# Seven-product v projection: first product in accumulator banks, phased sums of x, weight loads three tiles ahead, another store queue

## The chip, the cores and the metric

The kernel runs on one core of a Trainium2 chip. A core has a matrix engine (PE, with its weight loads PEld), three engines for element-wise work (DVE, ACT, POOL), and SP, which here only issues transfers. Each engine works through its own list of instructions in order and waits on semaphores for the others. The matrix engine writes to eight banks of PSUM of 128 x 512 float32, called bank 0 to 7 below. Transfers between the core's SBUF and DRAM are issued by SP or by ACT. The metric is device time in microseconds (us) of one execution.

## The reference

Two layers of a hybrid backbone run on 256 prompt tokens and 1024 sample tokens, 1280 rows of 1024 columns together, that is ten row tiles of 128. Layer 0 is a state-space mixer beside a convolution module; layer 1 is a chunked gating unit. The change lies at the start of layer 1:

```
u, v, gate = split(h @ w_in, 3)        # h: 1280 x 1024, w_in: 1024 x 6144
v = layer_norm(v)                      # over 2048 columns
s = per chunk and group: c_ws @ v + c_bs
y = (u * s * silu(gate)) @ w_out
x = layer_norm(ALPHA * x + gate_ada * y)
```

Everything is float32. h is x times (1 + scale) plus shift, with x the normalised output of layer 0. The part at hand is `v = h @ w_in[:, 2048:4096]`, 1280 x 1024 times 1024 x 2048, and the per-row statistics of v.

## The kernel before

**Float32 from two halves.** Each operand is split in two fp32r parts: a high part by a copy on ACT, a low part by a subtraction on DVE. A product is three matmuls: high x high, high x low, low x high.

**Seven products for eight.** The v projection uses a Strassen-like scheme (Winograd's form). The rows are halved (row tiles 0 to 4 and 5 to 9), the 1024 columns of x are halved (A11, A12, A22 and so on are such quarters of x), and the weights are taken in two passes p of two column blocks of 512, halved by rows. Each pass has seven products of a quarter, or a sum of quarters, with a weight block, or a difference of blocks, instead of eight. They run in the order `VORD = (1, 2, 5, 6, 7, 4, 3)`. A product is five steps, one for each row tile of the half; a step is 12 matmuls of 128x512 (4 pieces of the inner dimension, three matmuls each). Two passes of seven products of five steps make the loop `for step in range(70)` (line 1599), with m = step // 5 the number of the product and i = step % 5 the row tile. Products 6, 7 and 3 use sums of quarters of x: S2 = A21 + A22 - A11, S3 = A11 - A21 and S4 = A12 - S2, kept as split pairs.

**What a step does besides.** `v_post` (line 1571) takes the step's bank: ACT copies it, DVE adds it to an accumulator. `acc1` is five whole PSUM banks (3 to 7), `acc2` five buffers in SBUF. `mm_bank` hands out banks 0, 1, 2 in turn. Product 1 goes to a bank of `mm_bank`, and ACT copies it into `acc1[i]` (line 1573). Finished pieces of v get their statistics (`v_out`, line 1563, BN_STATS at 1564) and go to DRAM (vD) through ACT's queue (line 1565).

**Weights.** The first two products' weights come through an older stream (`W`, `wV`). For m from 2 to 13 each product has four `Item`s, k = 0 to 3, a 128x512 tile each: `load` (line 1462, SP, one or two sources of 256 KB), `comb` (line 1466, POOL takes the difference of two sources; for products 5 and 6 the difference is also stored to tD by SP, line 1468, since a later product needs it), and `split` (line 1473 ACT, 1474 DVE). A table `sched` puts the split of tile k of product m at step e = 5 (m - 1) + k, its comb at e - 1 and its load at e - 2. The raw tiles use a ring of five buffers, `hraw`.

**Sums of x.** The transposed rows of x were stored to xkD (line 1317) when they were made. `sum_load` and `sum_load2` read the quarters back (1408, 1409, 1412); `sums` (1422) forms S3 and S2 in part on POOL (1426, 1427) and DVE (1428, 1429), stores the fourth sum to sD (1430, SP) and splits S3 (1416, 1417); a second table at line 1627 splits S2. `S4Item` loads sD again and splits S4.

**The order of the work.** All of it is written out by hand: the program order of each engine is the order of the calls in the loop. After a step's matmuls come, in this order, the remaining transposes of row tiles 8 and 9 from layer 0 (`l8` and `l9`: PE line 324 into a bank, ACT line 1305, then POOL 1312 and 1316 and ACT 1315, and the xkD store), `v_post`, the splits, combs and loads of `sched`, and the sums. Waits follow from the buffers that instructions share. Ahead of the loop `fin0` finishes row tile 9 of layer 0: DVE reads its banks at line 1290, after splitting the first v weights at line 261.

## Time and profile before

| | |
|---|---|
| median of three runs | 2160.49 us (2158.58 to 2163.11) |
| profiled execution, its own time | 2159.95 us |
| its span, first to last instruction | 2158.2 us |
| mean granted PE clock | 0.965 |
| PE busy | 2014.7 us, 93% |
| DVE, ACT, POOL busy | 66%, 44%, 49% |
| the stage of the change | 1207.5 to 1481.8 us |

How to read it: the profile records each instruction's start and duration on its engine. Times are us from the span's start. "Idle before, releaser" says how long an engine stood still ahead of an instruction and whose completion ended that. `L209` is the helper that issues every matmul, so matmuls are told apart by the tiles they read. A granted clock of 0.50 means that matmuls ran at half speed. `SPq` and `ACTq` are the queues in which SP and ACT issue transfers; "to landing" is the time from issue to arrival. Names such as Flo, Fhi, Wr, Xa and Xb are buffers in SBUF, S4s is the area in which sums are formed, and ps is PSUM. The row tiles of x are in Rh (high) and Rl (low).

### The profile page before, as it was taken

What the parts mean: (1) busy time and instruction counts of PE and PEld (TensorE: products, weight loads), DVE (VectorE), ACT (ScalarE), POOL (GpSimd) and SP (SyncE); (2) the same over time, 40 slices, a digit from 0 to 9 for tenths busy, and PEclk for the clock granted to TensorE, in tenths of its full rate; (3) what the DMA queues carried; (4) which work ended last, traced back from release to release, by engine and by line L of the source; (5) the groups of instructions that cost most, each with busy time, mean ns of one, the idle gap of its engine ahead of it and who ended that gap; (6) DMA issues with size and microseconds to landing.
All of it is one profiled execution on the core that took longest, in us unless ns stands there. A gap on an engine that the chain in (4) does not pass through costs nothing.

```text
span 2158.2 us, 32301 instructions
## 1 busy us (share of the span) xinstructions
PE 2014.7 (93%) x12032; PEld 1781.0 (83%) x12032; DVE 1430.9 (66%) x2018; ACT 960.1 (44%) x1804; POOL 1050.2 (49%) x982
## 2 busy tenths in 40 slices
PE   7999999998989899899999767989999999989998
PEld 5788888878879788689988545768999999988987
DVE  5777888876795986966656436556555555555566
ACT  3555555567554554655544423333433333331221
POOL 3487788934654646526614433023444444445312
PEclk8999999999989999999999888999999999999999
DMA  8343421366423323244486356554323222265632
GB/s 333 106 137 113 150 77 57 96 191 189 120 73 101 108 78 113 94 152 153 156 274 211 132 194 198 179 183 149 94 93 94 93 94 93 69 226 179 205 129 86
DMA packets 183718, 300.62 MB, mean 139 GB/s; under 512 B 15536, under 2 KB 111992, under 8 KB 183560
## 3 DMA queue, kind: packets, MB, share of 16 engines
q1 hardware_dynamic: 139824, 256.69, 36.8%
q10 hardware_dynamic: 43736, 41.86, 5.7%
q8 instruction: 95, 1.56, 0.3%
q14 instruction: 63, 0.52, 0.1%
HBM read 218.35 MB, written 80.13 MB: 138 GB/s over the span
## 4 chain that ended last, share of the span: by engine, by line
PE 40%; DVE 9%; DMA 4%; POOL 3%; issue 3%; ACT 1%; SPq 1%; ACTq 0%; DVEq 0%; POOLq 0%
PE ps L209 40%; DVE X L914 1%; DVE Fhi L1148 1%; DMA Flo<-tD 1%; DMA Flo<-in_wv 1%; DVE Fhi L1291 1%; DVE Rl L320 1%; POOL Flo L1466 1%; DVE Fhi L901 1%; DVE Fhi L1292 1%; ACT Rh L319 0%; DVE Flo L685 0%; POOL X L865 0%; DVE Fhi L1290 0%; DVE Wr L261 0%
## 5 line engine op out<-in xcount | busy, mean ns | idle before, releaser
L209 PE MATMUL ps<-Rh,Wr 128*128 128x512 f32 (+2 forms) x2688 | 716.0, 352 | 3.9 <-ACT Rh L415 1.4
L209 PEld LDWEIGHTS ps<-Rh,Wr 128*128 128x128 f32 x2688 | 478.8, 193 | 69.2 <-issue 7.5
L209 PE MATMUL ps<-Rl,Wr 128*128 128x512 f32 (+2 forms) x1344 | 462.8, 349 | 1.8 <-DVE Rl L417 1.6
L209 PE MATMUL ps<-Wr,Rh 128*128 128x256 f32 (+2 forms) x1670 | 376.1, 316 | 34.8 <-DVE Fhi L1290 13.8
L596 POOL TENSOR_TENSOR X<-X 128x1295 f32<-128x1295 f32 x96 | 297.5, 3099 | 77.6 <-ACT X L594 72.1
L209 PEld LDWEIGHTS ps<-Wr,Rh 128*128 128x128 f32 x1670 | 276.1, 192 | 56.2 <-ACT Wr L1473 14.3
L209 PEld LDWEIGHTS ps<-Rl,Wr 128*128 128x128 f32 x1344 | 257.3, 192 | 29.9 <-DVE Rl L417 2.7
L209 PE MATMUL ps<-Wr,Rl 128*128 128x256 f32 (+2 forms) x854 | 267.0, 313 | 0.9 <-DVE Rl L320 0.8
L209 PEld LDWEIGHTS ps<-Wr,Rl 128*128 128x128 f32 x854 | 163.3, 191 | 10.6 <-DVE Rl L320 1.3
L590 DVE SCALAR_TENSOR_TENSOR ps<-Fhi,Flo,ps 128x1295 f32<-128x1295 f32 x102 | 160.0, 1569 | 2.9
L209 PE MATMUL ps<-Xa,Rh 128*128 128x512 f32 (+1 forms) x432 | 122.7, 359 | 3.9 <-DVE Xb L1733 2.5
L261 DVE TENSOR_TENSOR Wr<-Flo,Wr 128x1024 fp32r<-128x1024 f32 (+1 forms) x60 | 98.0, 1641 | 42.6 <-ACT Wr L259 42.6
L209 PE MATMUL ps<-Xb,Rh 128*128 128x512 f32 (+1 forms) x456 | 118.9, 350 | 1.3 <-ACT Xb L1473 1.1
L1466 POOL TENSOR_TENSOR Flo<-Flo 128x512 f32<-128x512 f32 x32 | 41.5, 1297 | 149.3 <-DMA Flo<-in_wv 72.4
L1148 DVE SCALAR_TENSOR_TENSOR Fhi<-Fhi,Flo 128x256 f32<-128x256 f32 (+2 forms) x144 | 109.2, 759 | 5.2 <-ACT Fhi L1144 0.8
L594 ACT ACTIVATE X<-Fhi,Flo 128x1295 f32<-128x1295 f32 x78 | 103.5, 1374 | 13.4 <-ACT Fhi L643 7.5
L220 POOL TENSOR_SCALAR Flo<-Flo 128x1 f32<-128x1 f32 (+1 forms) x31 | 11.9, 385 | 192.6 <-DVE Flo L686 186.6
L914 DVE SCALAR_TENSOR_TENSOR X<-X,Flo 128x128 f32<-128x128 f32 x160 | 92.5, 636 | 5.3 <-ACT X L911 3.6
L1528 ACT ACTIVATE Wr<-Flo 128x512 fp32r<-128x512 f32 x72 | 44.9, 624 | 114.8 <-PE ps L209 101.5
L209 PE MATMUL ps<-Xa,Rl 128*128 128x512 f32 (+1 forms) x252 | 91.5, 363 | 4.3 <-DVE Rl L320 4.3
L1529 DVE TENSOR_TENSOR Wr<-Flo,Wr 128x512 fp32r<-128x512 f32 x72 | 73.3, 1018 | 27.3 <-ACT Wr L1528 27.3
L209 PEld LDWEIGHTS ps<-Xa,Rh 128*128 128x128 f32 x432 | 77.4, 193 | 16.4 <-issue 2.8
(350 smaller groups left out, 4137.2 us busy)
## 6 DMA issues: line engine op xcount, KB each, us to landing
Fhi<-abD SPq DMA_DIRECT2D x80, 256.0 KB, 3.4
Fhi<-in_ada SPq DMA_DIRECT2D x34, 512.0 KB, 8.0
Flo<-in_wv SPq DMA_DIRECT2D x64, 256.0 KB, 3.7
Flo<-in_wug SPq DMA_DIRECT2D x32, 512.0 KB, 3.3
Flo<-in_wB SPq DMA_DIRECT2D x24, 512.0 KB, 3.3
Xb<-vD SPq DMA_DIRECT2D x15, 640.0 KB, 4.3
pD<-Xb SPq DMA_DIRECT2D x26, 320.0 KB, 2.5
Flo<-in_wA SPq DMA_DIRECT2D x16, 512.0 KB, 3.4
```

The lines of the kernel that those rows point to most:

```text
L209: PE.matmul(out=out, lhsT=a, rhs=b, start=st, stop=sp)
L261: e.tensor_tensor(out=l_, in0=r, in1=h_.bitcast(F32), op=SUB)
L320: eng.tensor_tensor(out=rl, in0=src, in1=rh.bitcast(F32), op=SUB)
L590: V.scalar_tensor_tensor(out=aD[:, 0:n], in0=u[:, k:k + n], scalar=wc(k), in1=aD[:, 0:n], op0=MULT, op1=ADD)
L594: S.activation(out=o[:, 0:n], in_=u[:, k:k + n], func=AF.Copy, scale=wc(k))
L596: G.tensor_tensor(out=aP[:, 0:n], in0=aP[:, 0:n], in1=o[:, 0:n], op=ADD)
L901: V.scalar_tensor_tensor(out=a[:, q], in0=a[:, q2], scalar=nA[:, sl(1, c)][:, h:h + 1], in1=a[:, q], op0=ADD, op1=MIN)
L914: V.scalar_tensor_tensor(out=cbd[:, q], in0=cbfb[:, 128:256], scalar=dt[:, sl(1, c)][:, h:h + 1], in1=cbd[:, q], op0=MULT, op1=ADD)
L1148: V.scalar_tensor_tensor(out=ob[:, a:e], in0=ib[:, a + k:e + k], scalar=w4(k), in1=ob[:, a:e], op0=MULT, op1=ADD)
L1466: G.tensor_tensor(out=self.r[0], in0=self.r[0], in1=self.r[1], op=SUB)
L1528: S.activation(out=w[:, 0:512], in_=src, func=AF.Copy)
L1529: V.tensor_tensor(out=w[:, 512:1024], in0=src, in1=w[:, 0:512].bitcast(F32), op=SUB)
```

## The change

Four things are changed, all in the loop of 70 steps.

- Product 1 is written straight into `acc1[i]`; its copy on ACT is gone, and `mm_bank` is not asked in those steps. The transposes of row tile 8 move from steps 1 and 2 to steps 2 and 3, those of row tile 9 from steps 3 and 4 to 6 and 7. The area for the sums is set up after step 7 instead of 4, and three statistics that were taken before it exists are copied over.
- The sums run in phases with tables of their own: `sum_load`, `sum_load2`, `sums` (POOL), `sums2` (DVE, and the split of S3), `sums3` (the sD store, and the split of S2). The fourth quarter of a round gets one of four places instead of a single one.
- The raw weight tiles are a first-in, first-out list: `load` takes buffers from its head, `split` gives them back. Two more buffers join at step 10. From m = 4 on a load is issued three steps ahead of its split, and its comb two steps.
- The store of a difference to tD is issued by ACT, after the split's copy, instead of SP.

```diff
+            def quarter(i):
+                m_ = 2560 + i % 2 * 1024
+                l_ = (4608, 2048, 4608, 0, 512)[i]
+                return (st[:, m_:m_ + 512], st[:, m_ + 512:m_ + 1024], st[:, i * 512:(i + 1) * 512], st[:, l_:l_ + 512])
+
             def sum_load(i):
...
             def sum_load2(i):
-                SP.dma_start(out=st[:, 4608:5120], in_=xkD[i, :, 512:1024])
+                a12 = quarter(i)[3]
+                SP.dma_start(out=a12, in_=xkD[i, :, 512:1024])
...
             def sums(i):
...
+                m0, m1, a11, _ = quarter(i)
                 G.tensor_tensor(out=m1, in0=m0, in1=m1, op=ADD)
                 G.tensor_tensor(out=m0, in0=a11, in1=m0, op=SUB)
+
+            def sums2(i):
+                m0, m1, a11, a12 = quarter(i)
                 V.tensor_tensor(out=a11, in0=m1, in1=a11, op=SUB)
                 V.tensor_tensor(out=a12, in0=a12, in1=a11, op=SUB)
+                to_sum(S3, i, m0)
+
+            def sums3(i):
+                _, _, a11, a12 = quarter(i)
                 SP.dma_start(out=sD[i], in_=a12)
-                to_sum(S3, i, m0)
+                to_sum(S2, i, a11)
...
                 def load(self):
-                    self.r = [next_raw() for _ in self.src]
+                    self.r = [hraw.pop(0) for _ in self.src]
...
                 def comb(self):
                     if len(self.r) == 2:
                         G.tensor_tensor(out=self.r[0], in0=self.r[0], in1=self.r[1], op=SUB)
-                        if self.keep is not None:
-                            SP.dma_start(out=self.keep, in_=self.r[0])
 
                 def split(self):
...
                     S.activation(out=h[:, c], in_=self.r[0], func=AF.Copy)
+                    if self.keep is not None:
+                        S.dma_start(out=self.keep, in_=self.r[0])
                     V.tensor_tensor(out=l[:, c], in0=self.r[0], in1=h[:, c].bitcast(F32), op=SUB)
+                    hraw.extend(self.r)
...
-                    self.r = next_raw()
+                    self.r = vtmp[self.i % 2]
                     SP.dma_start(out=self.r, in_=sD[self.i])
...
-                    at(e - 1, it.comb)
-                    at(e - 2, it.load)
-            for i, e in enumerate((19, 24, 26, 28, 29)):
+                    at(e - (1 if m < 4 else 2), it.comb)
+                    at(e - (2 if m < 4 else 3), it.load)
+            for i, e in enumerate((27, 28, 29, 30, 31)):
...
-                if j == 1:
-                    S.activation(out=acc1[i], in_=b, func=AF.Copy)
-                elif j == 2:
+                if j == 2:
...
+            vsv = F[:, FB - 70:FB - 52].rearrange("p (t n s) -> p t n s", n=1, s=6)
             for step in range(70):
...
+                    Wr.put(5 * WS, 6 * WS, (5 * WS, WS, sb.tile([128, WS], F32, name="Wr5f", tag="Wr5")))
+                    hraw += [Wr[:, 5 * WS + q * 512:5 * WS + 512 + q * 512] for q in range(2)]
...
-                b = mm_bank()
+                b = acc1[i] if j == 1 else mm_bank()
...
-                if step in (1, 2):
-                    l8(mm_bank, (step - 1,))
-                if step in (3, 4):
-                    l9(mm_bank, (step - 3,))
+                if step in (2, 3):
+                    l8(mm_bank, (step - 2,))
+                if step in (6, 7):
+                    l9(mm_bank, (step - 6,))
                 v_post(p, j, i, b[:, :])
-                if step == 4:
+                if step == 7:
                     st = sums_area()
...
-                for q in {11: (0, 1), 13: (2,), 15: (3,), 17: (4,)}.get(step, ()):
-                    to_sum(S2, q, st[:, q * 512:(q + 1) * 512])
-                if step in (7, 9, 11, 13, 15):
-                    sums((step - 7) // 2)
-                if step in (5, 7, 9, 11, 13):
-                    sum_load((step - 5) // 2)
-                if step in (5, 8, 10, 12, 14):
-                    sum_load2((step - 5) // 2)
-                if step == 17:
+                for f_, when in ((sums3, (12, 14, 15, 17, 18)), (sums2, (11, 13, 14, 16, 17)), (sums, (10, 12, 13, 15, 16)),
+                                 (sum_load2, (9, 11, 12, 14, 15)),
+                                 (sum_load, (8, 10, 11, 13, 14))):
+                    if step in when:
+                        f_(when.index(step))
+                if step == 18:
```

How this moves instructions, at two places. First SP's queue where the weights of the third product (m = 2) are loaded. Flo holds the raw weight tiles, in_wv is the weight in DRAM. Before:

```order
L1317 DMA xkD<-Fhi 128x1024 x2
L1462 DMA Flo<-in_wv 128x512 x2
L1317 DMA xkD<-Fhi 128x1024
L1468 DMA tD<-Flo 128x512
L1462 DMA Flo<-in_wv 128x512 x2
L1468 DMA tD<-Flo 128x512
L1462 DMA Flo<-in_wv 128x512 x2
```

And with the change, where line 1468 is the load:

```order
L1317 DMA xkD<-Fhi 128x1024 x2
L1468 DMA Flo<-in_wv 128x512 x8
L1317 DMA xkD<-Fhi 128x1024
L1468 DMA Flo<-in_wv 128x512
L1468 DMA Flo<-tD 128x512
L1414 DMA S4s<-xkD 128x1024
L1415 DMA S4s<-xkD 128x512
```

The stores to tD have left SP's queue, and eight loads stand together between the xkD stores of row tiles 8 and 9.

Second, ACT's queue from the last store of layer 0 (xhD) on. L1573 is the copy of the first product, L1305 the copy of transposed rows, L1581 the copy of the second product, L1477 the weight split. Before:

```order
L1298 DMA xhD<-Fhi 128x1024
L1573 ACTIVATE ps<-ps 128x512
L1305 ACTIVATE Fhi<-ps,Flo 128x128 x4
L1573 ACTIVATE ps<-ps 128x512
L1305 ACTIVATE Fhi<-ps,Flo 128x128 x4
L1315 ACTIVATE Rh<-Fhi 128x512
L1315 ACTIVATE Rh<-Flo 128x512
```

With the change:

```order
L1298 DMA xhD<-Fhi 128x1024
L1305 ACTIVATE Fhi<-ps,Flo 128x128 x8
L1315 ACTIVATE Rh<-Fhi 128x512
L1315 ACTIVATE Rh<-Flo 128x512
L1581 ACTIVATE Flo<-ps 128x512
L1572 DMA vD<-Flo 128x4x128
L1477 ACTIVATE Wr_65<-Flo 128x512
L1479 DMA tD<-Flo 128x512
```

The copies of the first product are gone, and the store to tD (L1479) stands behind the split of its tile, ahead of the next copies.

More of the change, by code (lines that the diff above doesn't have):

```diff
@@ L1593, in v_post @@
                     v_out(v, 5 + i, 2 * p)
[L1594 removed]
+                elif j == 3:
                     V.tensor_tensor(out=acc2[i], in0=b, in1=acc2[i], op=ADD)
```

16 lines of the change are left out of this document (6 added, 10 removed).

## The prediction

> **What bounds the kernel now.** I read the busy shares first: PE is busy for 93% of the span of 2158.2 us, so only a place where PE stands still can give much. Then stretches of the stage that the diff touches, from the last matmul before it (1207.5) to its last wait (1481.8); the columns are length, PE, weight loads, DVE, ACT, POOL, granted clock, DMA share, GB/s.
>
> ```profile
> 1207.50:1329.60 122.10, 71.20 (x258) 53.06 (x258) 51.40 (x74) 39.21 (x75) 41.27 (x35) 0.76 0.50 168
> 1329.60:1400.00 70.40, 70.40 (x305) 56.97 (x304) 45.33 (x69) 25.66 (x44) 8.47 (x7) 1.00 0.64 191
> 1329.60:1481.80 152.20, 142.90 (x602) 113.33 (x600) 92.10 (x140) 49.21 (x84) 30.19 (x24) 0.98 0.59 180
> 1207.50:1481.80 274.30, 214.10 (x859) 166.40 (x858) 143.49 (x214) 88.42 (x159) 71.46 (x58) 0.88 0.55 174
> ```
>
> Where nothing interrupts PE, 305 matmuls take 70.4 us: 0.231 us each, 2.77 us for a step of 12. The stage has 70 steps. Steps 0 to 19 (240 matmuls and 16 short transposes) would take 55.4 us and about 1.4 us; they take 122.1. Steps 20 to 69 would take 138.5; they take 152.2. So about 65 us stand in the first part and 14 in the second, and this is all that the change can win. What PE waits for, and what SP's queue waits for:
>
> ```profile
> PE ps L209 <- ACT Wr L1473: 20.0, 4, 10.0
> PE ps L209 <- DVE Fhi L1290: 13.8, 1, 13.8
> PE ps L209 <- ACT Fm L1580: 8.8, 2, 7.1
> PE ps L209 <- DVE Fm L1585: 8.3, 1, 8.3
> SPq L1468 <- POOL Flo L1466: 63.0, 16, 6.1
> SPq L1317 <- ACT Fhi L1305: 33.1, 3, 18.7
> ```
>
> PE waits for split weights (L1473), once for a bank (L1290), and for banks that ACT and DVE copy late (L1580, L1585). Behind the weights stands SP's queue: 16 stores to tD wait 63.0 us for POOL's differences, and loads stand behind them. The chain of waits shows one round:
>
> ```profile
> 1248.82 0.42 SPq L1462
> ...
> 1249.29 3.88 DMA Flo<-in_wv
> 1253.17 0.07 issue
> 1253.24 1.30 POOL Flo L1466
> 1254.55 0.33 SPq L1468
> 1254.88 0.04 issue
> 1254.92 0.43 SPq L1462
> ```
>
> Load, land, subtract, store, and only then the next load: 6.1 us for a weight tile, where PE's pace asks for one in 2.77. The late copies hang on the sums of x, since ACT runs in order and holds its queue at the split of a sum:
>
> ```profile
> ACT S L1416 <- POOL S4s L1427: 39.6, 5, 10.1
> L1426 POOL TENSOR_TENSOR S4s<-S4s x5: 1257/1261/1293, 1267.4 to 1315.2; 128x512 f32<-128x512 f32 x5
> ```
>
> Five rounds from 1267.4 to 1315.2: 12 us each.
>
> **The change, part by part.** I walked the new order of the queues with the durations of these rows.
>
> ```profile
> 1197.52 0.68 DVE L1290 TENSOR_TENSOR Fhi<-ps,Fhi 128x512 f32<-128x512 f32 x1
> 1207.40 1.22 DVE L261 TENSOR_TENSOR Wr<-Flo,Wr 128x1024 fp32r<-128x1024 f32 x1 [6.24 <-ACT Wr L259]
> 1221.00 0.42 DVE L1290 TENSOR_TENSOR Fhi<-ps,Fhi 128x256 f32<-128x256 f32 x1
> 1221.56 1.19 PE L209 MATMUL ps<-Wr,Rh 128*128 128x512 f32 x2 [13.85 <-DVE Fhi L1290]
> 1221.56:1226.82 5.26, 5.26 (x13) 4.15 (x13) 2.15 (x5) 1.24 (x1) 1.00 (x3) 0.50 0.00 0
> 1225.09 1.24 ACT L1297 ACTIVATE Fhi<-Fhi,Flo 128x1024 f32<-128x1024 f32 x1 [6.97 <-POOL Flo L690]
> 1233.69 1.50 ACT L1305 ACTIVATE Fhi<-ps,Flo 128x128 f32<-128x128 f32 x4 [1.23 <-PE ps L324]
> 1216.15 19.40 SPq L1317 DMA_DIRECT2D xkD<-Fhi  x2
> 1241.46 0.72 PE L209 MATMUL ps<-Xa,Rh 128*128 128x512 f32 x2
> 1275.15 0.63 PE L209 MATMUL ps<-Wr,Rl 128*128 128x512 f32 x1
> ```
>
> *First product into accumulator banks.* Ten ACT copies (L1573, 0.59 us each, 5.9 in all) go; beside PE they cost nothing, the bank does. Step 0 used bank 2, which DVE reads last at 1221.42. Bank 3, the new one, was last read at 1197.52 + 0.68, so step 0 waits only for its split weights, 1207.40 + 1.22: start 1208.7. Three steps end at 1217.0. The moved transposes of row tile 8 then need bank 2: again 1221.42, an idle time of 4.4 us. After the old idle time 13 matmuls ran at clock 0.50, 5.26 us for 3.0; I charge the same 2.3. Step 4 ends at 1221.5 + 2 x 2.77 + 0.8 + 2.3 = 1230.1; before, step 5 began at 1241.46. That is 11 us in hand.
>
> *Loads and the store queue.* ACT's L1297 (1225.09) doesn't move. Behind it eight copies of the transposes (twice 1.50, after a trigger) end at 1229.7 instead of 1233.69 + 1.50, so tile 8's xkD store, the second of L1317, leaves SP 5.5 us earlier and five loads follow it at once, about 0.45 apart. Costs of a weight tile from here:
>
> ```profile
> Flo<-in_wv SPq DMA_DIRECT2D x64, 256.0 KB, 3.7
> L1468 SPq DMA_DIRECT2D tD<-Flo x16: 319/323/327, 1248.4 to 1424.3; - x16
> DMA to landing us min/median/max: 2.0/2.0/2.0
> L1466 POOL TENSOR_TENSOR Flo<-Flo 128x512 f32<-128x512 f32 x32 | 41.5, 1297 | 149.3 <-DMA Flo<-in_wv 72.4 <-DMA Flo<-tD 36.0 <-DVE Wr L1474 34.9
> L1473 ACT ACTIVATE Wr<-Flo 128x512 fp32r<-128x512 f32 x24 | 15.1, 630 | 45.7 <-POOL Flo L1466 35.1 <-DVE Flo L1592 5.1 <-DVE Flo L1577 3.2
> L1474 DVE TENSOR_TENSOR Wr<-Flo,Wr 128x512 fp32r<-128x512 f32 x24 | 16.6, 694 | 38.1 <-ACT Wr L1473 36.0 <-DMA Flo<-in_wv 2.1
> L1565 ACTq DMA_DIRECT2D vD<-Flo x30: 366/366/393, 1248.5 to 1468.3; - x30
> ```
>
> The second load lands near 1234.5, so the first two differences are ready at 1235.8 and 1237.1. The price of the moved store: it is issued on ACT after the split (0.37 as L1565, 16 times, 5.9 us of ACT), and a raw buffer comes free only when its store has landed (2.0). Behind each trigger on ACT stand the next bank copies. So tiles 2 and 3 of the third weight set wait for 1239 and 1243.5, and are split by 1251 and 1254. Meanwhile step 9 waits for its bank: ACT's copy of step 7 writes a buffer that POOL's three operations for row tile 9 (1.3 each, from 1244.3) free at 1248.1. So step 9 runs from 1248.7 at half clock, step 10 ends at 1256.5 against 1275.6: 19 us in hand.
>
> *Sums in four phases.* A round no longer sits in one lump: loads of the next round leave while DVE still works on the last. But the transfers are many. From 1247 to the last sum there are 53 of 256 KB (20 of xkD, 19 of weights, 5 to sD, 9 to vD and tD).
>
> ```profile
> DMA packets 39171, 46.84 MB, mean 180 GB/s; under 512 B 2666, under 2 KB 22902, under 8 KB 39158
> q1 hardware_dynamic: 18275, 35.85, 43.1%
> q10 hardware_dynamic: 20883, 10.83, 14.0%
> ```
>
> 46.84 MB took 57.1% of 260 us, 148 us: 0.83 us for 256 KB when all engines work. So 53 x 0.83 = 44 us, to 1291. The walk through POOL (a difference and a sum pair, 3 x 1.3), ACT and DVE gives rounds that start on POOL at 1261, 1269, 1273, 1281 and 1286: 6 us each. The split of the last two S2 tiles now stands behind ACT's and DVE's work on steps 17 and 18, so that steps 18 and 19 each wait about 3 us (a copy of 0.6 and four DVE operations of 0.69 after the step before). Step 19 ends at 1296.5; the transfers alone would allow 1294. Before: 1329.6. 33 us.
>
> *Loads three tiles ahead, seven buffers.* For the second part: split (0.63), trigger (0.37), landing (2.0), load (0.4 + 3.7), difference (1.3), split again, with 0.4 for gaps: 8.8 us for three tiles or 2.9 for one. Five steps give 13.85 us for four tiles, 3.46 each. That fits, with 2 us in hand at the hardest place (steps 45 to 50), so of 152.2 there remain 138.5 + 2.3 for a start at half clock: 140.8, a gain of 11.4. If a landing takes 2 us more, this cover is gone and some 5 us return.
>
> Edits at nothing: the copy of three statistics (18 values) and the change of Wr5's use; DVE is idle for 131 of the 274 us here.
>
> *Sum:* 33 + 11.4 = 44, less 1 for the last bank wait and rounding: 43. The profiled execution took 2159.95, so 2117; the median of the runs, 2160.49, is 0.5 away. What follows the stage starts from the last vD stores and keeps PE full, so the gain should reach the end.
>
> A rule speaks against the new queue. The Trainium skill, page "DMA: Bandwidth & Descriptors", section "Rules for kernel authors": spreading transfers over SP and ACT gives no bandwidth and only saves the issuing sequencer's time. By it the move would be worth 16 issues of SP. The trace gives each store 0.32 us of issue (5.2 in all) and 63.0 us of waiting ahead of it, so the row says that more than issue is at stake; the rival that follows from the rule is the second below.
>
> **Rivals.** (1) *PE runs full after step 10.* If landings stay at 3.7 and the splits of S2 come in time, steps 11 to 19 take 9 x 2.77 and end at 1281.4: 15 us and the half clock less, 2100. For it: the DMA share of the stage was only 0.55. Against: the 53 transfers above, and the place of the late splits.
> (2) *Transfers set the pace, not the queue.* What was a wait in the queue becomes a longer landing: weights come no sooner, the five rounds stay at 12 us, the second part keeps its 14. Then the front's 11 us and the 5.2 of issue are left: 2144. For it: 0.64 DMA share even in a dense stretch. Against: the chain above has one transfer under way at a time.
> (3) *Slower: ACT is held by the stores.* If each of the 16 triggers keeps ACT until an older transfer has landed (3.7 us), bank copies stand behind it and PE gets 16 x 3.7 = 59 us of new waits against 43 won: 2176. It decides from 2.7 us for a trigger. Against: L1565 sits in the same queue and takes 0.37.
> (4) *The change doesn't do what it says:* the loads still wait, now for the store's landing and the split, as long as before: 2160.
>
> **How the numbers follow.** My forecast, 2117, has a chance of 0.60; (1) 0.16, (2) 0.16, (3) 0.05, (4) 0.03. The range takes in (1) and (2), that is the bounds of the unknown landing time: 2097 to 2146; the forecast's own is 2106 to 2130. A measurement of this kernel can't tell under 0.2% (4.3 us) from none. Faster 0.92, same 0.03, slower 0.05.
>
> **What would show it.** The first matmul of the stage at about 1208.7 and a wait for L1290 at its transposes; a wait of some 6 us at step 9 for ACT; no SP wait for POOL; sum rounds 6 us apart; step 19's end near 1296; steps 20 to 69 in 141 us at clock 1.00; DMA share near 0.9 from 1250 to 1290. Wrong if rounds stay 12 us apart, if ACT waits for transfers, or if idle time comes back in steps 45 to 58.

## The result and the profile after

| | before | after |
|---|---|---|
| median time (four runs each) | 2161.04 us | 2124.83 us (2123.77 to 2130.70) |
| ratio to before | | 0.984, 95% interval 0.982 to 0.986 |
| profiled execution, its own time | 2159.95 us | 2123.77 us |
| span | 2158.2 us | 2122.0 us |
| mean granted PE clock | 0.965 | 0.975 |

The change makes the kernel 36 us faster. The forecast was 43 us. The lines of the kernel have moved by a few: the load is now L1468, POOL's difference L1472, ACT's split L1477, the tD store L1479, DVE's split L1480; the sums are L1431 and L1432 on POOL, L1436 and L1437 on DVE; sums and S2 are split at L1423 (ACT) and L1424 (DVE); their loads are L1414, L1415 and L1419.

First the stretches of the stage of the kernel after (columns as in the prediction: length, PE, weight loads, DVE, ACT, POOL, granted clock, DMA share, GB/s). The cut at 1306 is the end of step 19.

```profile
1204.50:1306.00 101.50, 72.39 (x257) 54.31 (x256) 58.33 (x75) 37.19 (x70) 47.39 (x37) 0.80 0.61 211
1251.50:1306.00 54.50, 34.76 (x109) 24.76 (x108) 34.68 (x41) 15.31 (x27) 29.65 (x21) 0.72 0.70 243
1306.00:1445.60 139.60, 139.60 (x601) 112.74 (x600) 94.27 (x138) 47.19 (x79) 26.85 (x20) 1.00 0.62 189
1250.00:1290.00 40.00, 25.52 (x93) 18.88 (x91) 25.43 (x34) 13.05 (x23) 22.20 (x16) 0.82 0.85 296
```

Steps 20 to 69 now run without a gap: PE is busy for all of the 139.6 us, at full clock. Most of what is left to win, about 30 us, lies between 1251.5 and 1306, where 109 matmuls take 54.5 us. The timeline of PE shows where it stands still there and ahead of it (start, length, what, and in brackets the idle time before and its releaser):

```profile
1205.57 0.50 PE L209 MATMUL ps<-Wr,Rh 128*128 128x512 f32 x1 [0.76 <-DVE Wr L261]
1218.52 1.11 PE L324 MATMUL ps<-Flo,Fhi 128*128 128x128 f32 x4 [4.54 <-DVE Fhi L1290]
1244.12 0.73 PE L209 MATMUL ps<-Xa,Rh 128*128 128x512 f32 x2 [4.06 <-ACT Flo L1581]
...
1251.34 0.62 PE L209 MATMUL ps<-Wr,Rh 128*128 128x512 f32 x2
...
1262.20 0.40 PE L209 MATMUL ps<-Wr,Rl 128*128 128x512 f32 x1
1264.58 0.73 PE L209 MATMUL ps<-Xb,Xa 128*128 128x512 f32 x2 [1.98 <-ACT Xa L1423]
1269.66 8.15 PE L209 MATMUL ps<-Xb,Xa 128*128 128x512 f32 x22 [4.36 <-DVE Xa L1424]
1279.26 0.73 PE L209 MATMUL ps<-Xb,Xa 128*128 128x512 f32 x2 [1.45 <-ACT Xa L1423]
1281.54 2.54 PE L209 MATMUL ps<-Xb,Xa 128*128 128x512 f32 x10 [1.55 <-DVE Xa L1424]
1289.23 1.22 PE L209 MATMUL ps<-Xb,Xa 128*128 128x512 f32 x2 [5.15 <-ACT Xa L1423]
1293.67 4.64 PE L209 MATMUL ps<-Xb,Xa 128*128 128x512 f32 x10 [3.22 <-DVE Xa L1424]
1300.09 1.22 PE L209 MATMUL ps<-Xb,Xa 128*128 128x512 f32 x2 [1.78 <-ACT Xa L1423]
1301.57 4.63 PE L209 MATMUL ps<-Xb,Xa 128*128 128x512 f32 x10 [0.27 <-DVE Xa L1424]
```

Step 0 waits only for its split weights, the transposes wait once for L1290, step 9 once for a bank. Step 10 ends at about 1251.4, where step 11 begins; steps 11 to 14 run full to 1262.6. Then each wait is for S2 (tile Xa), first its high half, then its low half, and after most of them matmuls run slower than 0.231 us each. These eight waits add to 19.8 us.

In SP's queue of the kernel after, between 1225 and 1306, no wait for POOL is left (63.0 us in the whole kernel before). Apart from the end of one wait of an xkD store for ACT's copies of the transposes (L1305; over at 1226.8), what SP waits for now is a landed tD store and a finished split; the second fence has the landing times of tD and the five rounds on POOL.

```profile
SPq L1468 <- DMA tD<-Flo: 18.0, 5, 5.8
SPq L1414 <- DVE S L1424: 6.9, 2, 6.0
SPq L1442 <- DVE S4s L1437: 6.4, 2, 4.6
SPq L1419 <- DMA sD<-S4s: 4.6, 1, 4.6
```

```profile
L1479 ACTq DMA_DIRECT2D tD<-Flo x13: 326/338/509, 1233.5 to 1389.2; - x13
DMA to landing us min/median/max: 2.5/4.0/4.6
L1431 POOL TENSOR_TENSOR S4s<-S4s x5: 1262/1298/1735, 1259.1 to 1290.1; 128x512 f32<-128x512 f32 x5
```

The rounds start 31/4 = 7.75 us apart (12 before, 6 forecast). A store takes 4.0 us to land at the median; it took 2.0 before. The trace has the landing of only five of the 16 stores here and of one before, and why it grew is not shown: with the store back in SP's queue (store_on_sp below) it is 2.2 us, so more transfers beside it need not be the reason.

**Where the 36 us come from.** The profiled executions differ by up to 6 us in when the stage begins, without any change ahead of it. So I count from the end of the weight split on DVE that step 0 needs (L261; 1208.6 before, 1205.5 after), and to the last matmul of steps 10, 19 and 69.

| | before | after | gain | forecast |
|---|---|---|---|---|
| start to end of step 10 | 67.0 us | 45.9 us | 21.1 | 19 |
| steps 11 to 19 | 54.2 us | 54.8 us | -0.6 | 14 |
| steps 20 to 69 | 151.1 us | 139.7 us | 11.4 | 11.4 |
| ahead of the start | | | 3.1 | 0 |
| behind step 69 | | | 1.2 | -1 |
| sum | | | 36.2 | 43 |

So the front and the second part came about as forecast. Steps 11 to 19 did not: they were to take 40.0 us and take as long as before.

### The profile page after: what moved, and what is told of

Its sections match the earlier page's. It is cut to its first block, busy times and chain, and to the rows that moved or that the text cites. A ratio compares the mean times of both kernels' runs of the same rounds, so it can differ in the third digit from the quotient of the medians.

```text
span 2122.0 us, 32270 instructions
## 1 busy us (share of the span) xinstructions
PE 2011.8 (95%) x12032; PEld 1778.2 (84%) x12032; DVE 1441.4 (68%) x2019; ACT 956.5 (45%) x1794; POOL 1056.3 (50%) x982
## 4 chain that ended last, share of the span: by engine, by line
PE 44%; DVE 9%; POOL 2%; DMA 2%; issue 2%; ACT 1%; SPq 0%; ACTq 0%; DVEq 0%; POOLq 0%
PE ps L209 44%; DVE Fhi L1148 1%; DVE X L914 1%; DVE Fhi L1291 1%; DVE Rl L320 1%; DVE Fhi L1292 1%; DVE Fhi L901 1%; DVE Flo L685 0%; DVE Fhi L1290 0%; ACT Rh L319 0%; DMA Fm<-pD 0%; DMA Wr5f<-in_wv 0%; DMA Flo<-tD 0%; ACT Fhi L1297 0%; DMA y2D<-Fm 0%
## 5 line engine op out<-in xcount | busy, mean ns | idle before, releaser
L209 PE MATMUL ps<-Rh,Wr 128*128 128x512 f32 (+2 forms) x2432 | 657.9, 356 | 3.2 <-ACT Rh L415 1.4
L209 PEld LDWEIGHTS ps<-Rh,Wr 128*128 128x128 f32 x2432 | 436.0, 193 | 68.0 <-issue 6.2
L209 PE MATMUL ps<-Rl,Wr 128*128 128x512 f32 (+2 forms) x1216 | 423.0, 353 | 1.0 <-DVE Rl L417 1.0
L209 PE MATMUL ps<-Wr,Rh 128*128 128x256 f32 (+2 forms) x1628 | 354.9, 311 | 5.4 <-ACT Fhi L1110 2.3
L209 PEld LDWEIGHTS ps<-Wr,Rh 128*128 128x128 f32 x1628 | 265.3, 190 | 22.6 <-ACT Fhi L1110 2.5
L209 PEld LDWEIGHTS ps<-Rl,Wr 128*128 128x128 f32 x1216 | 233.3, 193 | 29.0 <-DVE Rl L417 1.9
L209 PEld LDWEIGHTS ps<-Wr,Rl 128*128 128x128 f32 x854 | 161.7, 189 | 10.5 <-DVE Rl L320 1.3
L261 DVE TENSOR_TENSOR Wr<-Flo,Wr 128x1024 fp32r<-128x1024 f32 (+1 forms) x60 | 97.9, 1639 | 42.8 <-ACT Wr L259 42.8
L209 PEld LDWEIGHTS ps<-Xb,Rh 128*128 128x128 f32 x456 | 78.6, 188 | 11.4
L908 ACT ACTIVATE Fhi<-Fhi,Flo 128x128 f32<-128x128 f32 x160 | 54.0, 392 | 73.4 <-DVE Fhi L901 64.7
L865 POOL TENSOR_TENSOR X<-X,Flo 128x256 f32<-128x256 f32 x72 | 53.7, 750 | 57.5 <-ACT X L862 39.1
```

What stands on the lines that cost most here:

```text
L209: PE.matmul(out=out, lhsT=a, rhs=b, start=st, stop=sp)
L261: e.tensor_tensor(out=l_, in0=r, in1=h_.bitcast(F32), op=SUB)
L865: G.tensor_tensor(out=h4(X2[c % 2] if i is None else XP[i % 3]), in0=h4(tk(c)[:, 0:256]), in1=bc(wd[:, sl(d, c)], 64), op=MULT)
L908: S.activation(out=a[:, q2], in_=a[:, q], func=AF.Exp, bias=nA[:, sl(0, c)][:, h:h + 1])
```

## Experiments

In all tables "step 19" is the time from the end of L261's split to the last matmul of step 19, and "20 to 69" the rest of the stage, both from the profiled execution; the ratio is to the kernel before, measured beside it (after: 0.984).

| kernel | median us | ratio, 95% interval | step 19 | 20 to 69 |
|---|---|---|---|---|
| before | 2161.04 | | 121.2 | 151.1 |
| after | 2124.83 | 0.984 (0.982 to 0.986) | 100.7 | 139.7 |
| front_only | 2150.88 | 0.996 (0.995 to 0.997) | 114.3 | 152.8 |
| store_on_sp | 2141.99 | 0.992 (0.990 to 0.993) | 110.2 | 146.8 |
| five_raw | 2129.88 | 0.986 (0.984 to 0.988) | 99.5 | 144.7 |
| sums_old | 2139.58 | 0.991 (0.989 to 0.992) | 115.2 | 139.4 |
| comb_dve | 2125.95 | 0.985 (0.984 to 0.986) | 101.5 | 139.4 |
| warm | 2124.34 | 0.984 (0.982 to 0.985) | 100.5 | 139.4 |
| less_xk | 2126.86 | 0.985 (0.983 to 0.986) | 100.6 | 139.4 |
| s2_first | 2116.30 | 0.981 (0.979 to 0.983) | 93.3 | 139.4 |
| sums_ahead | 2116.15 | 0.980 (0.979 to 0.981) | 89.7 | 139.4 |
| s2_split_phase | 2114.36 | 0.979 (0.977 to 0.981) | 91.2 | 139.4 |
| sum_loads_first | 2124.52 | 0.983 (0.981 to 0.985) | 100.0 | 139.4 |
| three_places | 2113.99 | 0.979 (0.977 to 0.981) | 88.3 | 139.6 |

### What each part is worth

**The front alone**, on the kernel before:

```diff
-                if j == 1:
-                    S.activation(out=acc1[i], in_=b, func=AF.Copy)
-                elif j == 2:
+                if j == 2:
...
-                else:
+                elif j == 3:
...
-                b = mm_bank()
+                b = acc1[i] if j == 1 else mm_bank()
```

> The kernel before with one part of the change: product 1 goes straight into the accumulator banks; transposes, sums, loads and the store queue stay as before. Theory (each part has its own place on the path): PE is some 11 us earlier after step 4, but the weights of the third product still come through SP's queue one at a time, so that only what the queue itself gains from the earlier last xkD store, 5 to 8 us, is left: about 2154. Rival (the weights' round of 6.1 us and the sums swallow it all): 2160, no change. Rival (the whole 11 us reach the end): 2149.

Measured: 2150.88 us, 8 us better by the ratio, between the theory and the rival that gave the whole 11. Step 19 ends 6.9 us earlier, within the 5 to 8 that the queue was to give. In step 10 PE waits for the weights as long as before (9.99 us there). From the waits and the timeline of PE in this kernel:

```profile
PE ps L209 <- ACT Wr L1473: 22.3, 4, 10.1
...
1265.54 1.52 PE L209 MATMUL ps<-Wr,Rh 128*128 128x512 f32 x2 [10.12 <-ACT Wr L1473]
```

From the start of the stage, step 10 begins 8.8 us earlier than in the kernel before (39.8 against 48.6) and step 11 still 6.9 us earlier. So most of what PE wins at the front gets through, because the weights of the third product come earlier too; but the long wait in step 10 stays.

**The store back in SP's queue:**

```diff
                 def comb(self):
                     if len(self.r) == 2:
                         G.tensor_tensor(out=self.r[0], in0=self.r[0], in1=self.r[1], op=SUB)
+                        if self.keep is not None:
+                            SP.dma_start(out=self.keep, in_=self.r[0])
...
-                    if self.keep is not None:
-                        S.dma_start(out=self.keep, in_=self.r[0])
```

> The changed kernel with the tD stores back in SP's queue, right behind POOL's difference. Theory (the wait in the queue was the cost): SP waits for POOL again, loads of weights and of the sums of x stand behind it, and some 15 us of the gain are lost: about 2140, with SP waits for POOL of 30 us or more. Rival (the queue gives only its issue time, 16 x 0.32 us, the rule of the Trainium skill that the prediction weighed): 2125 to 2130.

Measured: 2141.99 us, 17 us of the gain lost, 9.5 of them by step 19 and 7.1 behind it. SP's waits of this kernel between 1205 and 1320 show what holds the loads (L1474 is the store):

```profile
SPq L1474 <- POOL Flo L1472: 30.6, 7, 5.5
SPq L1474 <- POOL Wr5f L1472: 3.6, 1, 3.6
```

The queue's waits count, not its issue time: the move of 16 stores of 0.32 us (5.2 us together) is worth 17 us. The rule that the prediction weighed (the Trainium skill, "DMA: Bandwidth & Descriptors", section "Rules for kernel authors") is not contradicted on bandwidth, but that it "only saves sequencer issue time" doesn't hold here: a store that waits for POOL makes the loads behind it wait.

**Five raw buffers, every load two steps ahead:**

```diff
-                    at(e - (1 if m < 4 else 2), it.comb)
-                    at(e - (2 if m < 4 else 3), it.load)
+                    at(e - 1, it.comb)
+                    at(e - 2, it.load)
...
-                    hraw += [Wr[:, 5 * WS + q * 512:5 * WS + 512 + q * 512] for q in range(2)]
```

> The changed kernel with five raw buffers instead of seven and every load two steps ahead, every difference one step ahead. Theory (the second part gains by the longer lead): steps 20 to 69 go back from 140 towards 152 us, and steps 10 to 19 gain 1 to 3 us because the loads of the fifth product no longer stand between the sums: about 2135. Rival (the second part gains by the store queue alone, and the lead does nothing): 2122 to 2126.

Measured: 2129.88 us, 5 us lost, between the two. Steps 20 to 69 take 144.7 us instead of 139.7, and step 19 ends 1.2 us earlier. This stretch of the kernel, and the longest of PE's waits in it:

```profile
1308.30:1453.00 144.70, 142.06 (x602) 112.74 (x602) 91.12 (x138) 45.79 (x79) 27.78 (x22) 1.00 0.60 186
```

```profile
PE ps L209 <- DVE Xb L1480: 1.3, 2, 1.1
```

PE waits 2.6 us in all and is busy 2.5 us longer than in the kernel after (139.6). Of the second part's 11.4 us, 5.0 go without the longer lead (here) and 7.1 without the moved store (above): it needs both, and the two losses, 12.1 us together, come to about the whole.

**The sums in one lump again** (and, as these need the area for the sums earlier, the transposes at steps 1 to 4):

```diff
...
-                if step in (2, 3):
-                    l8(mm_bank, (step - 2,))
...
+                if step in (1, 2):
+                    l8(mm_bank, (step - 1,))
...
-                for f_, when in ((sums3, (12, 14, 15, 17, 18)), (sums2, (11, 13, 14, 16, 17)), (sums, (10, 12, 13, 15, 16)),
-                                 (sum_load2, (9, 11, 12, 14, 15)),
-                                 (sum_load, (8, 10, 11, 13, 14))):
-                    if step in when:
-                        f_(when.index(step))
+                for q in {11: (0, 1), 13: (2,), 15: (3,), 17: (4,)}.get(step, ()):
+                    to_sum(S2, q, st[:, q * 512:(q + 1) * 512])
+                if step in (7, 9, 11, 13, 15):
+                    sums((step - 7) // 2)
...
```

> The changed kernel with the sums of x as before: one lump for a round, one place for the fourth quarter, the transposes of row tiles 8 and 9 at steps 1 to 4. Theory (the phases bring the rounds closer): rounds some 12 us apart again, step 19 ends 14 to 19 us later: 2139 to 2144. Rival (rounds follow the weights' queue or the transfers, not the phases): 2125.

Measured: 2139.58 us, 15 us lost, all of it before step 20 (115.2 against 100.7). But only half of it is lost in steps 11 to 19, which take 62.0 us instead of 54.8. The other half is lost in step 10: it begins 4.6 us earlier than in the kernel after (38.4 against 43.0 from the start), and step 11 begins 7.4 us later (53.2 against 45.8). PE's wait there, and ACT's queue ahead of it, in this kernel:

```profile
1259.08 1.52 PE L209 MATMUL ps<-Wr,Rh 128*128 128x512 f32 x2 [9.28 <-ACT Wr L1470]
```

```profile
1255.28 0.63 ACT L1423 ACTIVATE S<-S4s 128x512 fp32r<-128x512 f32 x1 [7.00 <-POOL S4s L1432]
...
1258.39 0.63 ACT L1470 ACTIVATE Wr<-Flo 128x512 fp32r<-128x512 f32 x1 [2.00 <-DVE Flo L1575]
```

The split of the first sum (L1423) waits for POOL and holds ACT, and the weight split that PE needs stands behind it. The same wait stands in the kernel before and in front_only (9.99 and 10.12 us). So the phases, which start three steps later, are worth about 7 us in step 10 and 7 us in steps 11 to 19, and not the 14 that the forecast gave for steps 11 to 19. That steps 11 to 19 take as long as before (54.8 and 54.2 us), although the phases win 7 us in them, is because their front has become 21 us earlier and they would otherwise give a part of that back.

### Why steps 15 to 19 stay slow

Four suspects: PE's half clock, the shared work of DVE and POOL, the transfers, and the place of S2's split in the queues.

**PE kept busy** with matmuls that are thrown away:

```diff
+                for _ in range({15: 24, 17: 10, 18: 30, 19: 8}.get(step, 0)):
+                    mm(b[:, :], va(1, 0, 0)[0], wps[0][0][:, 0:512], True, True)
```

> The changed kernel with 24, 10, 30 and 8 more matmuls of 128x512 ahead of steps 15, 17, 18 and 19, into the bank that the step then overwrites; they fill the waits and compute nothing that is kept. Theory (after a wait PE runs at half clock, which cost 9.6 us in 109 matmuls between 1251.5 and 1306, and PE's late steps make ACT's copies late): the clock stays at 1.00, step 19 ends 4 to 7 us earlier: about 2119. Rival (the waits end when the splits are there, whatever PE does meanwhile): 2123 to 2126; the added matmuls themselves cost at most 72 x 0.231 = 16.6 us if they find no wait to fill.

Measured: 2124.34 us and the same step 19 (100.5). The stretch from 1250 to 1306 in this kernel:

```profile
1250.00:1306.00 56.00, 47.63 (x194) 35.93 (x192) 37.62 (x49) 17.80 (x31) 29.25 (x21) 0.98 0.76 254
```

The clock is at 0.98 instead of 0.73 (this execution starts 4 us later; from 1254 to 1310 it is 0.97), and nothing is won: a faster step only waits longer for the next split. The rival holds, and in steps 15 to 18 the half clock is a consequence, not the cause. One place the run leaves untested: behind its last wait, 2.55 us, the last ten matmuls of step 19 again take 4.14 us (4.63 in the kernel after, 2.31 at full speed). So some 2 us of half clock at the very end, an estimate from these figures, may be a price of their own.

**Differences of the fourth and fifth product on DVE:**

```diff
-                        G.tensor_tensor(out=self.r[0], in0=self.r[0], in1=self.r[1], op=SUB)
+                        (V if self.m in (3, 4) else G).tensor_tensor(out=self.r[0], in0=self.r[0], in1=self.r[1], op=SUB)
```

> The changed kernel with the weight differences of the fourth and fifth product on DVE (0.69 us alone) instead of POOL (1.3). Theory (beside a POOL operation a DVE operation on SBUF took 1.75 us instead of 0.69, eight times between 1259 and 1297, about 8 us, of which some 6 us stood ahead of S2's splits): DVE's operations there take 0.69 again, and with no difference ahead of the fourth round POOL starts it earlier: about 2117. Rival (DVE now waits for the weights' loads, and the bank sums stand behind it): 2130.

Measured: 2125.95 us, no gain. In this kernel the rounds begin on POOL at 1254.68, 1263.08, 1270.24, 1281.52 and 1287.98, which is 3 to 5 us earlier from the start than in the kernel after, and most of DVE's operations take 0.68 us again. But DVE now waits for weights ahead of the S2 splits. Rounds on POOL, and DVE on weights:

```profile
1281.52 1.35 POOL L1431 TENSOR_TENSOR S4s<-S4s 128x512 f32<-128x512 f32 x1 [8.66 <-DMA S4s<-xkD]
1287.98 1.38 POOL L1431 TENSOR_TENSOR S4s<-S4s 128x512 f32<-128x512 f32 x1 [3.43 <-DMA S4s<-xkD]
```

```profile
1273.84 0.69 DVE L1472 TENSOR_TENSOR Flo<-Flo 128x512 f32<-128x512 f32 x1 [3.65 <-DMA Flo<-in_wv]
```

The earlier round on POOL is eaten by a new wait in the next engine. This doesn't acquit the slow DVE operations, since the edit brought a cost of its own; it shows that an earlier POOL alone brings nothing.

**Fewer transfers**, six loads of x left out:

```diff
-                SP.dma_start(out=st[:, m_:m_ + 1024], in_=xkD[5 + i])
+                if i < 2:
+                    SP.dma_start(out=st[:, m_:m_ + 1024], in_=xkD[5 + i])
...
-                SP.dma_start(out=a12, in_=xkD[i, :, 512:1024])
+                if i < 2:
+                    SP.dma_start(out=a12, in_=xkD[i, :, 512:1024])
```

> The changed kernel without six of the fifteen loads of x's quarters (the pair of quarters and the fourth quarter of rounds three to five, 2.25 MB or nine pieces of 256 KB): these rounds compute with what lies there, so their sums and the parts of v made from them are left out of the right result; all operations stay. Theory (the transfers set the pace between 1250 and 1300, where the DMA engines are 85% busy): 9 x 0.83 = 7.5 us less at step 19, about 2117. Rival (the order of the queues and the latency of one round set it): rounds start at most 2 us earlier, 2122 to 2126.

Measured: 2126.86 us, nothing won with 2.25 MB less. POOL's rounds in this kernel (L1433 here; the fourth and fifth):

```profile
1281.27 1.72 POOL L1433 TENSOR_TENSOR S4s<-S4s 128x512 f32<-128x512 f32 x1
...
1291.13 1.36 POOL L1474 TENSOR_TENSOR Flo<-Flo 128x512 f32<-128x512 f32 x1 [6.45 <-DMA Flo<-in_wv]
1292.46 1.72 POOL L1433 TENSOR_TENSOR S4s<-S4s 128x512 f32<-128x512 f32 x1
```

From its start (1209.3) the fourth round comes at 72.0 instead of 78.9 us, 7 us earlier, yet step 19 ends at the same place. The fifth stands behind a weight difference that waits 6.45 us. The DMA share between 1250 and 1290 is down to 0.71 from 0.85. So neither these nine pieces of data nor one early round sets the end; the weights' loads, which the fifth round now waits behind, were not taken away.

**S2 split first**, S3 behind it:

```diff
             def sums2(i):
                 m0, m1, a11, a12 = quarter(i)
                 V.tensor_tensor(out=a11, in0=m1, in1=a11, op=SUB)
-                V.tensor_tensor(out=a12, in0=a12, in1=a11, op=SUB)
-                to_sum(S3, i, m0)
+                to_sum(S2, i, a11)
 
             def sums3(i):
-                _, _, a11, a12 = quarter(i)
+                m0, _, a11, a12 = quarter(i)
+                V.tensor_tensor(out=a12, in0=a12, in1=a11, op=SUB)
                 SP.dma_start(out=sD[i], in_=a12)
-                to_sum(S2, i, a11)
+                to_sum(S3, i, m0)
```

> The changed kernel with one reordering: S2 is split as soon as it is formed (in the second phase, one step earlier), S3 and the fourth quarter follow in the third phase; the number of operations is the same. Theory (steps 15 to 19 wait because the S2 split of a row tile stands behind the bank copies and weight splits of the step before, and PE's half clock after each wait makes those copies later still): step 18's row tile comes as soon as POOL has its sum, step 19 ends near 1298 instead of 1306: about 2117. Rival (the rounds on POOL and the transfers set the pace, the place of the split does not): 2123 to 2126.

Measured: 2116.30 us, as the theory had it. In this order the loads of rounds three to five come, in the program, ahead of the S3 splits of rounds one to three and overwrite their source: S3 of three row tiles is not the reference's, and these loads no longer wait for those splits. That may be a part of the gain, so the orders that follow don't have it.

**All computing phases ahead of the step's other work:**

```diff
+                for f_, when in ((sums3, (12, 14, 15, 17, 18)), (sums2, (11, 13, 14, 16, 17)), (sums, (10, 12, 13, 15, 16))):
+                    if step in when:
+                        f_(when.index(step))
                 v_post(p, j, i, b[:, :])
...
-                for f_, when in ((sums3, (12, 14, 15, 17, 18)), (sums2, (11, 13, 14, 16, 17)), (sums, (10, 12, 13, 15, 16)),
-                                 (sum_load2, (9, 11, 12, 14, 15)),
+                for f_, when in ((sum_load2, (9, 11, 12, 14, 15)),
```

> The changed kernel with the three computing phases of the sums (not the loads) called ahead of the bank copies, splits and differences of the same step. Theory (place in the queues): POOL forms a round before the difference of that step, so that the fourth round starts near 1281 instead of 1284, and ACT and DVE split S2 before they copy a bank: about 2117. Rival (the sums wait for their loads, and everything behind them on POOL, ACT and DVE now waits with them): 2128 to 2135, with PE waits for banks or weights.

Measured: 2116.15 us; step 19 ends 11.0 us earlier. PE's timeline in this kernel, with the idle times of over half a microsecond in steps 15 to 19:

```profile
1270.55 0.50 PE L209 MATMUL ps<-Xb,Xa 128*128 128x512 f32 x1 [1.07 <-ACT Xb L1477]
1275.98 5.30 PE L209 MATMUL ps<-Xb,Xa 128*128 128x512 f32 x16 [4.92 <-DVE Xb L1480]
...
1285.78 0.73 PE L209 MATMUL ps<-Xb,Xa 128*128 128x512 f32 x2 [1.59 <-ACT Xa L1423]
1290.86 7.71 PE L209 MATMUL ps<-Xb,Xa 128*128 128x512 f32 x22 [4.35 <-DVE Xa L1424]
```

Step 19's wait is gone (the last 22 matmuls run through), and step 15 waits for weights (Xb) instead, for 4.92 us: their low half now stands on DVE behind the second round.

**S2 in a phase of its own:** formed and split ahead of the bank copies; the fourth quarter and S3 behind the weight splits; POOL's round ahead of its difference.

```diff
                 V.tensor_tensor(out=a11, in0=m1, in1=a11, op=SUB)
+                to_sum(S2, i, a11)
+
+            def sums2b(i):
+                m0, _, a11, a12 = quarter(i)
                 V.tensor_tensor(out=a12, in0=a12, in1=a11, op=SUB)
                 to_sum(S3, i, m0)
 
             def sums3(i):
-                _, _, a11, a12 = quarter(i)
-                SP.dma_start(out=sD[i], in_=a12)
-                to_sum(S2, i, a11)
+                SP.dma_start(out=sD[i], in_=quarter(i)[3])
...
+            W2 = (11, 13, 14, 16, 17)
...
+                if step in W2:
+                    sums2(W2.index(step))
                 v_post(p, j, i, b[:, :])
...
-                for f in [f for f in fs if f.__name__ == "split"] + [f for f in fs if f.__name__ == "comb"] + [f for f in fs if f.__name__ == "load"]:
+                for f in [f for f in fs if f.__name__ == "split"]:
                     f()
+                if step in W2:
+                    sums2b(W2.index(step))
+                if step in (10, 12, 13, 15, 16):
+                    sums((10, 12, 13, 15, 16).index(step))
+                for f in [f for f in fs if f.__name__ == "comb"]:
+                    f()
...
```

> The changed kernel in a new order, nothing left out: S2 is formed and split ahead of the bank copies of its step; then bank copies and weight splits; then the fourth quarter and the split of S3; POOL forms a round ahead of its weight difference; the loads keep their order. Theory (the place in DVE's and ACT's queues costs the time): only two DVE operations of a round stand ahead of the weight splits, so that the wait of 4.9 us for a weight split, which the order with all phases ahead had, goes too: step 19 ends some 12 us earlier than in the changed kernel: about 2112. Rival (transfers set the pace): no better than the order with all phases ahead, 2116, or worse.

Measured: 2114.36 us, between the two, and not to be told apart from the last one by time. The 4.92 us wait is gone, but step 15 still waits 6 us for weights in three pieces, and step 18 for S2:

```profile
1267.35 0.73 PE L209 MATMUL ps<-Xb,Xa 128*128 128x512 f32 x2 [2.09 <-DVE Xb L1482]
1270.70 0.80 PE L209 MATMUL ps<-Xb,Xa 128*128 128x512 f32 x1 [2.62 <-ACT Xb L1479]
1272.84 8.04 PE L209 MATMUL ps<-Xb,Xa 128*128 128x512 f32 x26 [1.34 <-DVE Xb L1482]
1285.50 1.22 PE L209 MATMUL ps<-Xb,Xa 128*128 128x512 f32 x2 [4.62 <-ACT Xa L1423]
```

**The same, with the loads of the sums ahead of the weight loads:**

```diff
-                for f in [f for f in fs if f.__name__ == "load"]:
-                    f()
                 for f_, when in ((sums3, (12, 14, 15, 17, 18)), (sum_load2, (9, 11, 12, 14, 15)), (sum_load, (8, 10, 11, 13, 14))):
                     if step in when:
                         f_(when.index(step))
+                for f in [f for f in fs if f.__name__ == "load"]:
+                    f()
```

> The same new order, and SP issues the loads of the sums ahead of the weight loads of the same step. Theory (SP's queue holds a load of x behind weight loads that wait for a landed tD store, 22 us in six waits): rounds start 2 to 5 us earlier, but weights come up to 1 us later per round: about 2109. Rival (the weights become late instead): 2114 to 2120, with PE waits for weight splits in steps 11 to 19.

Measured: 2124.52 us, worse than the rival's range: the whole gain of the new order is gone. From SP's waits and PE's timeline in this kernel:

```profile
SPq L1414 <- DVE S L1424: 15.1, 3, 9.8
SPq L1445 <- DVE S4s L1441: 12.4, 2, 6.8
```

```profile
1280.48 0.79 PE L209 MATMUL ps<-Xb,Xa 128*128 128x512 f32 x1 [6.49 <-ACT Xb L1479]
```

A sum's load waits for a split two rounds back, and now the weights stand behind that wait. It is the same fault as the tD store in the kernel before, with the roles exchanged.

**More room for the sums**, on the order with S2 in its own phase: the third round's pair in the buffer of the bank copies (xc), fourth quarters where no store has just left, S3 ahead of the fourth quarter.

```diff
             def quarter(i):
-                m_ = 2560 + i % 2 * 1024
-                l_ = (4608, 2048, 4608, 0, 512)[i]
...
+                mp = xc if i == 2 else st[:, 2560 + i % 2 * 1024:3584 + i % 2 * 1024]
+                l_ = (4608, 0, 512, 4608, 1024)[i]
...
-                V.tensor_tensor(out=a12, in0=a12, in1=a11, op=SUB)
                 to_sum(S3, i, m0)
+                V.tensor_tensor(out=a12, in0=a12, in1=a11, op=SUB)
...
-                for f_, when in ((sums3, (12, 14, 15, 17, 18)), (sum_load2, (9, 11, 12, 14, 15)), (sum_load, (8, 10, 11, 13, 14))):
+                for f_, when in ((sums3, (12, 14, 15, 17, 18)), (sum_load2, (9, 11, 13, 14, 15)), (sum_load, (8, 10, 11, 13, 14))):
```

> The order with S2 split in its own phase (2114 us), and the sums get more room: the third round's pair of quarters goes to the buffer that holds bank copies from step 15 on, so that the fourth and fifth round's loads wait for the S3 split of a round that is three back instead of two; the fourth quarters lie where no store to sD has just left; S3 is split ahead of the fourth quarter's subtraction; the third round's fourth quarter is loaded one step later. Theory (a round's loads wait in SP's queue for the S3 split two rounds back, 7.0 us in three waits, and for a landed sD store, 5.0 us): these waits go, the fourth and fifth round start on POOL 2 to 5 us earlier, step 19 ends some 3 us earlier: about 2111. Rival (the weights of the fourth product, late by 6 us in step 15, and the landing of the loads set it now): 2113 to 2117.

Measured: 2113.99 us, in the rival's range; step 19 ends 3.0 us earlier in the profiled execution, as the theory had it, but the time can't tell the two kernels apart. The load's wait for S3 (7.0 us in three waits before) no longer stands in SP's list, a new one does (L1417, the load of a fourth quarter, for DVE's subtraction), and the fourth round still waits on POOL for its load:

```profile
SPq L1417 <- DVE S4s L1440: 9.9, 2, 7.0
```

```profile
1281.00 1.29 POOL L1429 TENSOR_TENSOR S4s<-S4s 128x512 f32<-128x512 f32 x1 [4.11 <-DMA S4s<-xkD]
```

The two best kernels, 2114 us, beat the kernel after by 10 us; their intervals (0.977 to 0.981) don't touch that of the kernel after (0.982 to 0.986).

**What sets the end of step 19, read across these runs.** The table follows the fifth row tile, from the timelines of POOL, DVE and PE; times are us from the end of L261's split.

| kernel | fifth round starts on POOL | ends on POOL | its S2 split done on DVE | step 19 ends |
|---|---|---|---|---|
| after | 84.6 | 87.5 | 96.0 | 100.7 |
| comb_dve | 81.7 | 84.4 | 97.5 | 101.5 |
| less_xk | 83.2 | 86.2 | 96.4 | 100.6 |
| s2_first | 81.6 | 84.9 | 90.5 | 93.3 |
| sums_ahead | 75.6 | 79.0 | 86.7 | 89.7 |
| s2_split_phase | 78.6 | 81.5 | 87.0 | 91.2 |
| sum_loads_first | 87.3 | 90.7 | 95.4 | 100.0 |
| three_places | 77.7 | 80.7 | 85.7 | 88.3 |

In every one of them step 19 ends 2.6 to 4.7 us behind that split. Two things move the split: when the round ends on POOL, and how long its sum then passes through the queues of DVE and ACT (8.5 us in the kernel after). S2 ahead of S3 shortens the passage to 5.6 us, its own phase to 5.5; this is worth about 3 us. The rest of what the better orders win is that the rounds end earlier on POOL: 6.0 us in s2_split_phase and 8.5 in sums_ahead, where the passage is hardly shorter (7.7). comb_dve has an earlier round but a longer passage, sum_loads_first a short passage but a late round, and neither wins. So the place of S2's split is a part of the cause, not the whole. Why the rounds come earlier in the better orders (POOL's own order, or loads that are let go sooner because S3 is split sooner) no run separates.

## Why the prediction was right, and where not

**The front and the loads: right.** Step 0 starts when its weights are split, the transposes wait 4.54 us (forecast 4.4), step 9 waits 4.06 us for ACT's copy (forecast about 6), step 10 has 21 us in hand (19). The prediction booked all of it with the banks, the loads and the store queue. The runs divide it otherwise: by the end of step 10 front_only has 6.9 us of the 21, putting the store back takes 3.8 away (step 11 begins at 49.6 instead of 45.8), and the sums in one lump take 7.4 away, since the first sum's split then holds ACT in front of a weight split. So a third of this gain hangs on the sums.

**The store queue: right in direction and mechanism.** SP no longer waits for POOL, and putting the store back costs 17 us. One size was off: the landings that the trace has are 4.0 us at the median, not 2.0. I had written that 2 us more would take the cover from the second part and return 5 us. It didn't: steps 20 to 69 have no wait at all. That reserve was larger than my sum for three tiles said. (Its first comparison, a tile every 2.77 us, was too strict besides: four tiles for five steps make 3.46, as the later sum has.)

**Sums in four phases: the term that was mis-sized.** The step was the walk to "step 19 ends at 1296.5": from step 10 it gave 40.0 us, and it took 54.8. This is 14.8 us, about the part of the sums term that went beyond step 10. Its parts, from the start of the stage: the fifth round began on POOL at 84.6 us, where the walk had 77.3 (1286 less 1208.7); and from there to the end of step 19 it took 16.1 us, where the walk had 10.5. So 7.3 us are late rounds, 7.75 us apart where the walk had 6, and 5.6 us are late splits. I had charged steps 18 and 19 a wait of 3 us each and the others none; the waits for S2 are 6.3 us in step 15, 3.0 in 17, 8.4 in 18 and 2.1 in 19, and in step 19 ten matmuls then take 4.63 us instead of 2.31. What the walk left out is that S3 and the fourth quarter go ahead of S2 in DVE's queue, though S2 is needed five steps sooner. Four orders that bring S2's split forward on the same data (s2_first with the reservation named, sums_ahead, s2_split_phase, three_places) end step 19 7 to 12 us earlier, at 88 to 93 us; the forecast had 87.9. A fifth, sum_loads_first, does not, since its loads come late; and by the table above more of the gain is earlier rounds than an earlier split.

**Transfers and clock in that term.** Beside the walk I had set the transfers as a second bound (53 x 0.83 us) and expected a DMA share near 0.9. The share was 0.85, but taking nine of the 53 pieces away changed nothing, so these at least did not bind. The half clock, which I had left out of these steps, costs nothing measurable in steps 15 to 18: at 0.98 instead of 0.73 step 19 ends at the same place. At its last ten matmuls it may cost some 2 us, which no run tests.

**Steps 20 to 69: right.** 139.7 us against the forecast's 140.8, at full clock. Both the lead and the moved store are needed for it.

**The rivals.** (1), PE full after step 10, 2100: fell, with 19.8 us of waits; the best order found ends step 19 at 88.3, where full speed would be near 71 (45.9 + 9 x 2.77). (2), only issue time, 2144: fell by the store put back, 17 us against 5. (3), ACT held by triggers: fell, a trigger takes 0.34 us at the median and 0.51 at most. (4) fell with the result.

**Luck in the total.** The two profiled executions put the start of the stage 3.1 us earlier after than before, and the starts of all kernels here spread over 6 us. Without that the gain of the stage and what follows it is 33 us of the 43. Front and tail came 2 us better each than forecast; with the early start this makes up half of the 14.6 us that steps 11 to 19 fell short.

**What stays open.** Why step 15 still waits 6 us for weights in the better orders is not settled: weights, rounds and stores share SP's queue and wait for each other's landings, and moving either ahead delayed the other. Nor is it settled why a store issued by ACT lands later than one issued by SP. I did not try an order with the weight differences of the fourth product ahead of the second round, nor keeping the tD differences in SBUF.

## What to carry to other kernels

A transfer that waits for a computing engine belongs in no queue that loads stand behind; what it costs there is the wait, not the issue, and moving it can be worth three times its issue time. When several results are formed in one round, split first the one that is needed first, and put it ahead of work that waits for the engine you are feeding; but look also at when its inputs come, which here was worth more. Before calling a wait's companions its cause (a low clock, busy transfers), take each away by itself: here a full clock in four of the five steps and nine transfers less changed nothing. When an experiment loses what a part was forecast to win, look also where it loses it.

## What the runs showed of the hardware

A DVE operation with both inputs in SBUF takes up to 1.81 us beside one on POOL, where the prediction's 0.69 us is that of one alone. From the timelines of DVE and POOL of the kernel after:

```profile
1262.11 1.75 DVE L1436 TENSOR_TENSOR S4s<-S4s 128x512 f32<-128x512 f32 x1 [1.19 <-POOL S4s L1432]
1263.89 0.69 DVE L1437 TENSOR_TENSOR S4s<-S4s 128x512 f32<-128x512 f32 x1
...
1266.19 0.68 DVE L1586 TENSOR_TENSOR Fm<-ps,Fm 128x512 f32<-128x512 f32 x1
```

```profile
1262.03 1.28 POOL L1472 TENSOR_TENSOR Flo<-Flo,Wr5f 128x512 f32<-128x512 f32 x1
...
1265.68 1.72 POOL L1431 TENSOR_TENSOR S4s<-S4s 128x512 f32<-128x512 f32 x1
```

L1436 starts 0.08 us behind a POOL operation, ends 0.55 us after it and takes 1.75 us; L1437, with POOL idle, takes 0.69. L1586, which reads one operand from PSUM, takes 0.68 in the midst of a POOL operation. The same holds for all such operations between 1255 and 1446: the 17 with two SBUF inputs that start behind a POOL operation still running end 0.54 or 0.55 us after it, whenever they started, and the 25 with one operand in PSUM beside POOL all take 0.68 to 0.69 us. This agrees with the Trainium skill, page "SBUF — State Buffer", section "Who interferes with whom": a DVE instruction with two SBUF inputs contends with a GpSimd (here POOL) instruction that reads SBUF, for a pair of ports that only one of them can hold at a time, and one with at most one SBUF input doesn't contend.
